# A two-block transformer layer stack on one core: the engines' instruction order drawn up on a detailed timeline instead of a simple clock

## The chip, the core and the metric

The kernel runs on one core of one Trainium2 chip. A core has a matrix engine (TensorE, called PE in the profile, with its weight loads shown apart as PEld), VectorE (DVE), ScalarE (ACT), GpSimd (POOL) and SyncE (SP), which here issues every transfer from memory. The metric is the device time of one execution in microseconds (us); lower is better. The time given for a kernel is the median of several executions.

## What is computed

256 tokens of width 1024 pass through a first block and then through two layers of a second block, all in 32-bit floats:

```
x = first_block(x, ...)       # norm, one wide projection, three mixers side by side
                              # (gated recurrence, sparse attention, gated linear attention),
                              # gated merge, output projection, feed-forward
return second_block(x, c, ctx, ...)   # two layers over 256 tokens and 256 context tokens:
                              # half feed-forward, mixer (attention + gating, or pooling +
                              # neighbourhood attention), half feed-forward
```

In the second block every norm is scaled and shifted by vectors that come from a small input through a large matrix:

```
m = jnp.split((sc @ ada_w[li] + ada_b[li])[:, None, :], N_MOD, axis=-1)
```

Each layer uses 9 such vectors for the tokens and 9 for the context. Nearly all the arithmetic is in products with weight matrices, each of which is read once.

## The kernel before

**Matmuls.** A weight tile is 128 by 1024 floats (512 KB). `wload` (L62 to L78) loads it into `wraw`, ScalarE rounds it to a shorter format (`wh`, L71), and VectorE computes what the rounding left out (`wl`, L72). `mm3` (L99) then multiplies with both parts: for each 128-column piece of a tile one product with `wh` (L104) and one with `wl` (L105), and after these the product of `wh` with the small part of the activations (L108). A full tile gives 24 matmuls. `wraw`, `wh` and `wl` have three buffers each, the PSUM tiles four of tag `mm` and four of tag `at` (L96).

**Work beside it.** The modulation vectors are made on VectorE. `Ada.chunk` (L1059) loads 128 by 512 floats into `araw` and multiplies and sums them twice (`junk`, L1066), once for the tokens and once for the context. There are 288 chunks. They are "fillers": `wload` calls `fill` at a rate that the stage sets, so that some chunks are written down after each weight tile. `junk` shares the tag `silu`, with two buffers, with the feed-forward's intermediate results.

**Norms.** A norm sums squares (L148 to L152), adds them up over partitions with small matmuls (`rstd`, L164), takes a power on GpSimd (L116), spreads the result with transposes (L173), and scales the activations on VectorE and ScalarE (L185 to L195) before the next projection can start. `stagger` (L198) splits the tokens in halves at most such places, so that one half's matmuls run while the other half is normed. The last mixer (`out_proj` with 256 tokens) doesn't split; there two weight tiles are loaded ahead, with their `wl` computed on GpSimd.

**Attention.** `weave` (L218) writes down a step of an attention chain after each so many dense matmul units.

**What sets the order.** The Python code writes instructions down in one sequence, the program order. When the `TileContext` (L2012) is left, a scheduler walks a clock of its own and draws up a list for each engine: when an engine is free on that clock, it gets the instruction that stands earliest in program order among those whose inputs are ready and whose tile has a buffer. Buffers of a tag are handed out in program order. On the chip each engine then runs its list in that order, and semaphores make an instruction wait for its inputs. So program order is a priority, and the scheduler's clock decides what overtakes what.

## Time and profile before

| quantity | value |
|---|---|
| median of 3 executions | 2399.82 us |
| lowest, highest | 2396.43, 2409.7 us |
| the profiled execution: its time | 2397.43 us |
| the profiled execution: its span, first to last instruction | 2395.7 us |
| TensorE busy | 2356.5 us, 98% of the span |
| VectorE busy | 1715.2 us, 72% |
| ScalarE busy | 1049.3 us, 44% |
| GpSimd busy | 183.7 us, 8% |
| mean clock granted to TensorE, share of full | 0.990 |
| moved by transfers | 398.91 MB |

Busy time is the time in which at least one instruction of an engine was running. The times of rows are those of the profiled execution, which took 1.7 us more than its span. [...]

### The profile page before, as it was taken

How to read it: one execution, taken by the hardware profiler on the slowest of the kernel's cores; microseconds unless marked ns; L12 is line 12 of the kernel's file. 1: busy time of each engine (PE TensorE's matmuls, PEld its weight loads, DVE VectorE, ACT ScalarE, POOL GpSimd, SP SyncE). 2: the span in 40 equal slices, each digit the busy share in tenths (PEclk: the TensorE clock that was granted, in tenths of full speed). 3: DMA queues.
4: the chain of work that ended last, by engine and by line, in shares of the span. 5: the costliest groups of instructions: out<-in, count | busy, mean ns of one | idle time of the engine just before them, and what ended most of it. 6: DMA issues, size and time to landing. Idle time of an engine off the chain costs nothing.

```text
span 2395.7 us, 38691 instructions
## 1 busy us (share of the span) xinstructions
PE 2356.5 (98%) x14647; PEld 2072.7 (87%) x14647; DVE 1715.2 (72%) x3622; ACT 1049.3 (44%) x1879; POOL 183.7 (8%) x208
## 2 busy tenths in 40 slices
PE   8999999999999999999999999999999999998999
PEld 8888988999999988888778888889888888878999
DVE  6986798679899965448787765666865655856555
ACT  4542576565444532236755322224422223665443
POOL 1100130010000000013321000000100000101000
PEclk8999999999999999999999999999999999998999
DMA  7884534367887754555324644544654543633655
GB/s 215 271 270 129 154 100 127 124 191 226 255 260 215 243 183 139 149 168 167 99 67 140 209 150 133 159 146 141 205 163 123 167 137 106 185 100 117 190 181 156
DMA packets 158022, 398.91 MB, mean 167 GB/s; under 512 B 27099, under 2 KB 41339, under 8 KB 157835
## 3 DMA queue, kind: packets, MB, share of 16 engines
q1 hardware_dynamic: 157835, 396.44, 53.1%
q8 instruction: 115, 1.88, 0.3%
q14 instruction: 72, 0.59, 0.1%
HBM read 389.56 MB, written 5.77 MB: 165 GB/s over the span
## 4 chain that ended last, share of the span: by engine, by line
PE 88%; DVE 5%; DMA 2%; ACT 2%; POOL 2%; issue 1%; SPq 0%; ACTq 0%; DVEq 0%; POOLq 0%
PE ps_mm L104 24%; PE ps_mm L105 24%; PE ps_mm L108 24%; PE ps_mm L1208 2%; PE ps_mm L1210 2%; PE ps_mm L1209 2%; DVE wl L72 1%; PE ps_at L1325 1%; PE ps_mm L1457 1%; PE ps_mm L578 1%; PE ps_at L1314 1%; ACT wh L71 1%; DMA wraw<-in_up 1%; DVE junk L1066 1%; PE ps_mm L1687 1%
## 5 line engine op out<-in xcount | busy, mean ns | idle before, releaser
L71 ACT CAST wh<-wraw 128x1024 fp32r<-128x1024 f32 (+2 forms) x603 | 604.7, 1004 | 754.6 <-PE ps_mm L108 383.1
L72 DVE TENSOR_TENSOR wl<-wraw,wh 128x1024 fp32r<-128x1024 f32 (+2 forms) x601 | 706.6, 1177 | 294.7 <-ACT wh L71 287.9
L104 PE MATMUL ps_mm<-zh,wh 128*128 128x256 f32 (+1 forms) x2568 | 769.2, 324 | 7.9 <-ACT wh L71 3.9
L105 PE MATMUL ps_mm<-zh,wl 128*128 128x256 f32 (+1 forms) x2568 | 766.8, 323 | 3.1 <-DVE wl L72 3.0
L104 PEld LDWEIGHTS ps_mm<-zh,wh 128*128 128x128 f32 x2568 | 492.5, 192 | 61.8 <-issue 12.0
L105 PEld LDWEIGHTS ps_mm<-zh,wl 128*128 128x128 f32 x2568 | 493.2, 192 | 45.4 <-DVE wl L72 5.3
L108 PE MATMUL ps_mm<-zl,wh 128*128 128x256 f32 (+1 forms) x2568 | 455.7, 320 | 0.0
L108 PEld LDWEIGHTS ps_mm<-zl,wh 128*128 128x128 f32 x2568 | 381.6, 190 | 38.1 <-issue 1.0
L1066 DVE SCALAR_TENSOR_TENSOR junk<-araw,cs 128x512 f32<-128x512 f32 x576 | 391.0, 693 | 11.1 <-DMA araw<-in_ada_w 3.7
L104 PE MATMUL ps_mm<-hh,wh 128*128 128x256 f32 (+1 forms) x1021 | 312.3, 328 | 0.9 <-ACT wh L71 0.9
L105 PE MATMUL ps_mm<-hh,wl 128*128 128x256 f32 (+1 forms) x1021 | 310.9, 327 | 1.1 <-DVE wl L72 1.1
L104 PEld LDWEIGHTS ps_mm<-hh,wh 128*128 128x128 f32 x1021 | 192.2, 188 | 21.1 <-ACT wh L71 1.1
L105 PEld LDWEIGHTS ps_mm<-hh,wl 128*128 128x128 f32 x1021 | 192.3, 188 | 19.8 <-DVE wl L72 1.5
L108 PE MATMUL ps_mm<-hl,wh 128*128 128x256 f32 (+1 forms) x1021 | 193.6, 327 | 0.0
L263 ACT ACTIVATE silu<-ps_mm 128x256 f32<-128x256 f32 (+1 forms) x124 | 58.7, 473 | 303.8 <-PE ps_mm L108 287.9
L108 PEld LDWEIGHTS ps_mm<-hl,wh 128*128 128x128 f32 x1021 | 156.2, 188 | 18.3 <-DVE hl L266 0.3
L1155 DVE SCALAR_TENSOR_TENSOR X<-ps_mm,adac,X 128x256 f32<-128x256 f32 x128 | 61.8, 483 | 129.2 <-PE ps_mm L108 127.6
L264 DVE TENSOR_TENSOR silu<-silu,ps_mm 128x256 f32<-128x256 f32 (+1 forms) x124 | 65.9, 531 | 110.9 <-PE ps_mm L108 110.1
L116 POOL TENSOR_TENSOR rs_v<-rs_v,power 128x2 f32<-128x2 f32 (+1 forms) x17 | 22.6, 1331 | 1068.3 <-ACT wh L71 692.1
L1208 PE MATMUL ps_mm<-wh,zh 128*128 128x512 f32 (+1 forms) x224 | 87.0, 389 | 0.0
L1209 PE MATMUL ps_mm<-wh,zl 128*128 128x512 f32 (+1 forms) x224 | 85.4, 381 | 0.0
L1210 PE MATMUL ps_mm<-wl,zh 128*128 128x512 f32 (+1 forms) x224 | 85.3, 381 | 0.0
(379 smaller groups left out, 2611.1 us busy)
## 6 DMA issues: line engine op xcount, KB each, us to landing
wraw<-in_up SPq DMA_DIRECT2D x204, 512.0 KB, 3.7
araw<-in_ada_w SPq DMA_DIRECT2D x288, 256.0 KB, 3.5
wraw<-in_w_in_t SPq DMA_DIRECT2D x72, 512.0 KB, 4.0
wraw<-in_dn SPq DMA_DIRECT2D x79, 448.0 KB, 3.2
wraw<-in_f_up SPq DMA_DIRECT2D x44, 512.0 KB, 4.1
wraw<-in_dn SPq DMA_DIRECT2D x40, 512.0 KB, 3.7
wraw<-in_ev_in SPq DMA_DIRECT2D x26, 512.0 KB, 4.3
wraw<-in_w_br SPq DMA_DIRECT2D x24, 512.0 KB, 3.6
```

Of the source, the lines that this page charges most:

```text
L71: nc.scalar.copy(h[:, :cols], raw[:, :cols])
L72: (low or nc.vector).tensor_tensor(out=l[:, :cols], in0=raw[:, :cols], in1=h.bitcast(F32)[:, :cols], op=ALU.subtract)
L104: nc.tensor.matmul(out, wh, ah, start=start and k == 0, stop=False)
L105: nc.tensor.matmul(out, wl, ah, start=False, stop=False)
L108: nc.tensor.matmul(out, wh, al, start=False, stop=stop and k == n - 1)
L263: nc.scalar.activation(g, pair[0], AF.Silu)
L264: nc.vector.tensor_tensor(out=g, in0=g, in1=ps, op=ALU.mult)
L1066: nc.vector.scalar_tensor_tensor(out=junk, in0=raw, scalar=1.0, in1=self.cs[:, s, h * 512:(h + 1) * 512], op0=ALU.mult, op1=ALU.mult, accu ...
L1155: self.nc.vector.scalar_tensor_tensor(out=X[:, m, :], in0=ps, scalar=self.ada.c[l][:, j, m, s:s + 1], in1=X[:, m, :], op0=ALU.mult, op1=AL ...
L1208: nc.tensor.matmul(ps[i], z.zh[:, k, tk], wh[:, w], start=k == 0, stop=False)
L1209: nc.tensor.matmul(ps[i], z.zl[:, k, tk], wh[:, w], start=False, stop=False)
L1210: nc.tensor.matmul(ps[i], z.zh[:, k, tk], wl[:, w], start=False, stop=k == 7)
```

## The change

One argument is added. The kernel's own code, its tiles, buffers and instructions are those of before.

```
     out = nc.dram_tensor("out", (P, 8, 256), F32, kind="ExternalOutput").ap()
-    with tile.TileContext(nc) as tc:
+    with tile.TileContext(nc, schedule_with_timeline_sim=True) as tc:
         build(tc, D, out)
```

The scheduler's rule stays: earliest in program order among those that are ready. What changes is the clock on which it decides who is ready and who is free. The simple clock gives each instruction one duration on its engine. The detailed one follows an instruction through its engine's sequencer, its waits, its execution and the signal that it sends, and lets transfers share the transfer engines.

## Rows read from the trace of the kernel before

**Rows 1.** The page: span, busy time by engine, chain that ended last.

```profile
span 2395.7 us, 38691 instructions
...
PE 2356.5 (98%) x14647; PEld 2072.7 (87%) x14647; DVE 1715.2 (72%) x3622; ACT 1049.3 (44%) x1879; POOL 183.7 (8%) x208
...
PE 88%; DVE 5%; DMA 2%; ACT 2%; POOL 2%; issue 1%; SPq 0%; ACTq 0%; DVEq 0%; POOLq 0%
```

**Rows 2.** Windows of 60 us: PE, PEld, DVE, ACT, POOL, clock, DMA, GB/s.

```profile
0.00:60.00 60.00, 52.26 (x343) 49.60 (x344) 40.38 (x86) 28.42 (x47) 7.58 (x22) 0.86 0.71 215
60.00:120.00 60.00, 56.15 (x378) 50.78 (x377) 55.71 (x125) 34.99 (x48) 6.22 (x7) 0.94 0.84 270
...
480.00:540.00 60.00, 57.28 (x462) 56.38 (x461) 44.93 (x81) 36.35 (x70) 11.80 (x14) 0.97 0.62 193
...
600.00:660.00 60.00, 60.00 (x501) 59.79 (x500) 50.94 (x103) 27.10 (x42) 0.00 (x0) 1.00 0.82 255
...
720.00:780.00 60.00, 57.92 (x482) 57.16 (x481) 54.42 (x118) 28.85 (x45) 1.39 (x2) 1.00 0.72 218
...
900.00:960.00 60.00, 60.00 (x260) 48.65 (x259) 36.05 (x73) 14.98 (x19) 0.00 (x0) 1.00 0.47 144
...
1260.00:1320.00 60.00, 56.71 (x372) 51.23 (x372) 48.26 (x101) 35.22 (x69) 9.03 (x10) 0.97 0.47 145
...
2160.00:2220.00 60.00, 52.15 (x401) 50.66 (x401) 40.06 (x77) 32.45 (x66) 9.67 (x7) 0.89 0.43 132
...
2340.00:2395.70 55.70, 52.09 (x434) 51.70 (x432) 28.18 (x37) 20.45 (x29) 0.00 (x0) 1.00 0.50 152
```

**Rows 3.** Waits of PE: for whom, total us, times, longest.

```profile
PE ps_at L173 <- POOL rs_v L116: 6.1, 5, 2.0
PE ps_at L164 <- DVE acc L152: 5.6, 1, 5.6
PE ps_mm L104 <- ACT wh L71: 4.9, 6, 2.0
PE ps_mm L105 <- DVE wl L72: 4.1, 8, 0.9
```

**Rows 4.** Timeline of the first 14 us: start, length, engine, operation.

```profile
1.59 0.56 POOL L826 MEMSET gatt<- 128x256 f32 x2
...
10.43 1.04 ACT L71 CAST wh<-wraw 128x1024 fp32r<-128x1024 f32 x1 [0.30 <-DMA wraw<-in_w_in_t]
...
12.81 0.87 DVE L185 SCALAR_TENSOR_TENSOR zt<-X,ng,ps_at 128x256 f32<-128x256 f32 x2 [1.35 <-PE ps_at L173]
...
13.61 1.22 DVE L72 TENSOR_TENSOR wl<-wraw,wh 128x1024 fp32r<-128x1024 f32 x1
```

**Rows 5.** Timeline around the norm after the last mixer, 2186 to 2196 us.

```profile
2187.17 0.43 DVE L152 TENSOR_TENSOR acc<-acc,sq 128x256 f32<-128x256 f32 x1
...
2189.74 4.84 POOL L72 TENSOR_TENSOR wl<-wraw,wh 128x1024 fp32r<-128x1024 f32 x2 [123.77 <-ACT wh L71]
2190.01 2.36 DVE L152 TENSOR_TENSOR acc<-acc,sq 128x256 f32<-128x256 f32 x1 [1.55 <-ACT sq L151]
...
2192.69 2.17 DVE L152 TENSOR_TENSOR acc<-acc,sq 128x256 f32<-128x256 f32 x1
```

**Rows 6.** Groups of instructions: busy us, mean ns, idle before.

```profile
L71 ACT CAST wh<-wraw 128x1024 fp32r<-128x1024 f32 (+2 forms) x603 | 604.7, 1004 | 754.6 <-PE ps_mm L108 383.1
L72 DVE TENSOR_TENSOR wl<-wraw,wh 128x1024 fp32r<-128x1024 f32 (+2 forms) x601 | 706.6, 1177 | 294.7 <-ACT wh L71 287.9
...
L1066 DVE SCALAR_TENSOR_TENSOR junk<-araw,cs 128x512 f32<-128x512 f32 x576 | 391.0, 693 | 11.1 <-DMA araw<-in_ada_w 3.7
...
L1066 DVE DVE_READ_ACCUMULATOR junk<-araw,cs 128x1 f32 x576 | 47.6, 83 | 0.0
```

**Rows 7.** Windows of line 1066 alone: DVE busy (instructions), clock, DMA, GB/s.

```profile
180.00:240.00 60.00, 16.51 (x50) 0.97 0.41 128
240.00:300.00 60.00, 0.00 (x0) 1.00 0.51 154
```

## Prediction

> **What bounds the kernel now.** I read the page first. PE is busy in 2356.5 of 2395.7 us and makes up 88% of the chain that ended last [rows 1]. No instruction is added or taken away, so this work stays: an order can only act on the 39.2 us in which PE stands still, on the time in which its clock is low after such stops, and on new stops.
>
> The windows of 60 us say where the 39.2 us lie [rows 2]. The first window has 7.74 (60 less 52.26), the one from 2160 us has 7.85, and the last has 3.61. At the first and the last there is little beside the one chain of loads, norm or output, so I call these three, 19.2 us together, set by the dependencies (with one exception below). The other 20.0 us are open to an order: 3.85 in 60 to 120, 2.72 in 480 to 540, 2.08 in 720 to 780, 3.29 in 1260 to 1320, and the rest in pieces. [...] In the windows between, as 900 to 960, PE is busy throughout at 1.00, and no order can speed that up.
>
> The waits of PE name the causes [rows 3]: the power on GpSimd in a norm (6.1 us), the sums of squares (5.6 in one wait), and weights that came late, rounded part 4.9 and rest 4.1.
>
> **How far the order can move.** The trace shows that the lists do not follow program order. GpSimd clears tiles of the linear attention (L826) at 1.59 us, though the code writes them after most projections [rows 4]. But buffers bind it. The fillers (L1066) take 16.51 us of VectorE in 180 to 240 and none in 240 to 300 [rows 7]: the next ones are written after the first tiles of tag `silu` of the second block, and that tag is handed out in program order. Weight tiles can't run more than three ahead, PSUM tiles four of a tag. So the new clock can swap neighbours; it can't move work between stages.
>
> **The change, part by part.**
>
> *Misjudged arrivals.* An example is in the start: ScalarE has the second weight tile rounded at 11.47 us (10.43 + 1.04). VectorE stands still until 12.81, does two products of the norm, and only then takes the rest `wl`, 1.22 us, after which the other products of the norm follow [rows 4]. The list was drawn up on a clock on which the tile came later. Had `wl` come first, it would have run in the 1.35 us of idle time, and the norm's chain would be up to 1.2 us shorter. A clock that describes transfers more closely may repair this: between 0 and -1.2 us, and I take -1.2. The late weights, 9.0 us together [rows 3], are of the same kind. A better clock could remove all of them; equally, one transfer that lands later on the chip than on any clock leaves them. I take a third, -3.0.
>
> *Non-preemptive fillers.* An engine's list can't be interrupted on the chip. Where a chain step becomes ready just after a filler was placed, it waits for the rest of it. A chunk takes 1.32 us of VectorE (16.51 us for 25 pairs of product and accumulator read, two pairs a chunk, [rows 7]), a `wl` 1.18 [rows 6]. At the five norms where PE waited for GpSimd [rows 3], two VectorE steps stand in the chain. If the new order puts one half of 1.2 us more before half of these steps, that is 5 x 0.6 = 3.0 us; the bounds are a gain of the 6.1 us waited now and a loss of 5 x 2 x 1.32 = 13.2. I take +3.0, nearer to zero, since the same rule of priority holds.
>
> *The norm after the last mixer.* There VectorE's sums (L152) take 2.36 and 2.17 us instead of 0.43, while GpSimd runs two `wl` in 4.84 us [rows 5]. Without the collision the chain is 2.36 + 2.17 - 2 x 0.43 = 3.7 us shorter, half of the 7.85 us of idle time there. The clock of this window is 0.89, up to 6.6 us more [rows 2]. This is the exception named above. The order could keep the two apart, by putting GpSimd's work before or after. But both `wl` are ready as soon as ScalarE has rounded the tiles, GpSimd has nothing else to do, and the rule starts what is ready. So I take 0 here; the bounds are -10.3 (3.7 and 6.6) and nothing.
>
> [...]
>
> *PE's own list.* Swapping matmuls that are ready leaves their sum as it is: nothing, covered by PE's own backlog of up to three tiles. Where that cover is gone, it shows as one of the waits above.
>
> *Sum.* -1.2 - 3.0 + 3.0 + 0 = -1.2 us, from 2397.4 (span 2395.7 and 1.7 around it) to 2396.2. The median of the runs was 2.4 us above the profiled one, so I expect a median of 2399.
>
> **The rivals.**
>
> *Slower: VectorE's lists get too full in the tight stages.* In 60 to 120 VectorE is busy 55.71 of 60, in 600 to 660 50.94, in 720 to 780 54.42 [rows 2]; a tile passes PE in 24 x 60/501 = 2.87 us. If the detailed clock fills an engine's queue ahead of time, it decides sooner and with fewer candidates ready, so fillers overtake `wl` more often. What it takes: three buffers give a tile 3 x 2.87 = 8.6 us from rounding to its last matmul; rounding, rest and matmuls need 1.00 + 1.18 + 2.87 = 5.05 [rows 2, 6]. So 3.5 us are spare: two chunks (2.64) in front of a `wl` are hidden, three (3.96) are not. From there each tile that is late costs its whole further delay, and a VectorE at 90% hardly catches up. The stages 60 to 180 and 540 to 840 pass 420/2.87 = 146 tiles; one in six late by a chunk is 24 x 1.32 = 32 us, 2431. It decides from nine such tiles on (12 us). For it: PE already waits for `wl` eight times. Against it: each wait is 0.9 us or shorter [rows 3], and PE is not idle at all in 600 to 660.
>
> [...]
>
> [...]
>
> *Nothing happens: the orders come out nearly the same.* Then 2399.8 stays. For it: long stretches of full tiles with one possible order.
>
> **How the numbers follow.** A difference of 0.5%, 12 us, is about what a measurement of this kernel can tell from none. Within it: 0.44, of which 0.06 for orders nearly alike; the likeliest case has its own range, 2389 to 2411. Slower: 0.31, nearly all from full lists on VectorE; I give it more than the sum suggests since new stops have no upper bound, while only 27 to 37 us can be won. Faster: 0.25. The range from 2382 to 2432 leaves out one in ten on each side: below, more than half of all that an order can give; above, more than one late tile in six.
>
> **What would show it.** Right: PE busy near 2356 us, idle time between 30 and 50 us, fillers in the same stages as now, the stops at 0 to 22 and 2185 to 2200 us still there. The first step is right if `wl` of the second tile starts before 12 us. Fullness shows as waits of PE for `wl` and `wh` of more than 15 us together, in 60 to 180 and 540 to 840. Wrong would be a changed PE busy time, long new waits in the attention stages (PE for `n`, `t` or `ysb`), which I count as hidden, or fillers that appear in 240 to 540.

## The result, and the profile after

The changed kernel takes 2442.1 us (median of 4 runs, 2438.6 to 2452.7) against 2403.5 for the kernel before: a ratio of 1.0175, 95% interval 1.0151 to 1.0198. It is slower by 1.75%; the forecast was no change, and the time lies 10 us above the range.

The page of the kernel after, to be held against [rows 1]:

```profile
span 2438.2 us, 38759 instructions
...
PE 2370.3 (97%) x14647; PEld 2083.6 (85%) x14647; DVE 1710.3 (70%) x3622; ACT 1051.1 (43%) x1879; POOL 172.8 (7%) x208
```

PE runs the same 14647 matmuls, and the other engines as many instructions as before; the 68 more are semaphore instructions. The span is 42.5 us longer: PE stands still for 67.9 us instead of 39.2 (28.7 more), and its busy time grows by 13.8. The clock can account for the second part: the mean granted clock fell from 0.990 to 0.982, at most 0.008 x 2438 = 20 us.

The waits of PE, kernel after, to be held against [rows 3]:

```profile
PE ps_mm L104 <- ACT wh L71: 12.3, 18, 1.5
PE ps_at L164 <- DVE acc L152: 5.7, 2, 5.5
PE ps_at L173 <- POOL rs_v L116: 5.2, 3, 2.2
PE ps_mm L104 <- ACT zh L194: 5.2, 3, 2.9
PE ps_mm L1208 <- ACT zh L190: 5.1, 2, 2.6
PE ps_mm L105 <- DVE wl L72: 4.9, 7, 1.4
PE ps_mm L104 <- ACT zh L190: 4.7, 3, 1.9
PE ps_at L1314 <- ACT n8u L1286: 3.6, 3, 2.0
```

Rows of the kernel before that [rows 3] doesn't have:

```profile
PE ps_mm L104 <- ACT zh L190: 2.8, 3, 1.1
...
PE ps_mm L104 <- ACT zh L194: 1.1, 1, 1.1
```

Two things have grown: the rounded weights `wh` come late 18 times instead of 6, and PE waits longer for steps on ScalarE, the norm's tiles `zh` (15.0 us in the rows above, 3.9 before) and the even layer's attention (`n8u`, 3.6; `n`, 1.9 before). The rest of a weight, `wl`, is hardly later than before at line 105.

To see where the time went I cut both traces at the same places, the matmuls of line 173 (and 890) with which a norm begins to broadcast its result. The windows that matter, kernel before (length, PE busy, granted clock, DMA share, GB/s): the first projections, the first block's attention, the stage with tiles of 256 columns, the even layer, the odd layer's mixer.

```profile
0.00:236.70 236.70, 225.09 (x1486) 0.94 0.70 224
236.70:511.70 275.00, 271.58 (x2060) 1.00 0.44 136
511.70:779.20 267.50, 263.99 (x2183) 0.99 0.74 231
...
1099.20:1303.50 204.30, 198.28 (x1083) 0.99 0.35 110
...
2055.40:2197.90 142.50, 135.80 (x747) 0.98 0.44 135
```

The same five, kernel after:

```profile
0.00:243.50 243.50, 227.26 (x1542) 0.96 0.70 220
243.50:515.30 271.80, 269.73 (x2045) 0.99 0.44 139
515.30:799.10 283.80, 272.72 (x2218) 0.98 0.71 223
...
1123.40:1337.90 214.50, 200.98 (x1063) 0.94 0.33 101
...
2093.60:2241.20 147.60, 134.97 (x728) 0.95 0.38 118
```

The stage with 256 columns is 16.3 us longer, the even layer 10.2, the first projections 6.8, the odd mixer 5.1. (A cut is no fence: 35 matmuls more lie in the longer 256-column stage, so a few of its us are moved work.) The long stretches of 512 columns between them, 1072 us before, lose 8 us together, and the end gains 0.8.

What happens in the 256-column stage, at its start. Start and end of three weight tiles in PE, us (from both traces, each matmul matched with its tile by its place in PE's list):

| tile | before | after |
|---|---|---|
| `ps_mm_1175` | 518.55 to 525.12 | 517.47 to 531.91 |
| `ps_mm_1176` | 519.90 to 528.19 | 517.71 to 532.03 |
| `ps_mm_1183` | 528.62 to 531.70 | 519.29 to 532.75 |

The new list has all three begun by 519.29 us, and they end within 0.84 us of each other. The three slots of `wh` and `wl` are taken for 13 us and then come free together. What follows, timeline of the kernel after (start, length, engine, operation, idle time before it):

```profile
531.95 0.38 ACT L263 ACTIVATE silu<-ps_mm 128x256 f32<-128x256 f32 x1 [5.91 <-PE ps_mm L108]
532.23 1.98 ACT L71 CAST wh<-wraw 128x1024 fp32r<-128x1024 f32 x2
...
533.00 2.44 DVE L1740 SCALAR_TENSOR_TENSOR n<-n,ng,ps_at 128x256 f32<-128x256 f32 x6 [0.22 <-PE ps_at L173]
...
533.32 0.38 PE L104 MATMUL ps_mm<-zh,wh 128*128 128x256 f32 x1 [0.35 <-ACT wh L71]
...
534.26 0.38 PE L104 MATMUL ps_mm<-zh,wh 128*128 128x256 f32 x1 [0.56 <-DVE n L1740]
534.39 1.04 ACT L71 CAST wh<-wraw 128x1024 fp32r<-128x1024 f32 x1
...
535.48 0.38 PE L104 MATMUL ps_mm<-zh,wh 128*128 128x256 f32 x1 [0.84 <-ACT wh L71]
...
536.63 0.58 PE L105 MATMUL ps_mm<-zh,wl 128*128 128x256 f32 x1 [0.77 <-DVE wl L72]
```

ScalarE stood still for 5.91 us and now has three tiles to round in 3.2 us; VectorE takes the first `wl` only after six steps of the norm, 2.44 us. The three matmuls of line 104 are the first of three further tiles, and only then comes the second matmul of the first one: PE's list again begins a tile, leaves it, begins the next, and stands still for 2.5 us in four waits.

In PE's list of the kernel before, PE leaves an unfinished tile of the weight stream for another one 157 times, in the new list 473 times (counted in the lists themselves); of the 533 tiles of `mm3`, 56 and 214 have a matmul of another PSUM tile between their own. Of the 157 and 473 changes, 12 and 59 stand in the 256-column stage.

### The profile page after: what moved, and what is told of

It is laid out like the page before. It is cut to its first block, busy times and chain, and to the rows that moved or that the text cites. A ratio compares the mean times of both kernels' runs of the same rounds, so it can differ in the third digit from the quotient of the medians.

```text
span 2438.2 us, 38759 instructions
## 1 busy us (share of the span) xinstructions
PE 2370.3 (97%) x14647; PEld 2083.6 (85%) x14647; DVE 1710.3 (70%) x3622; ACT 1051.1 (43%) x1879; POOL 172.8 (7%) x208
## 4 chain that ended last, share of the span: by engine, by line
PE 63%; DVE 2%; ACT 2%; DMA 1%; issue 0%; POOL 0%; ACTq 0%; DVEq 0%; POOLq 0%
PE ps_mm L104 17%; PE ps_mm L105 17%; PE ps_mm L108 17%; PE ps_mm L1208 2%; PE ps_mm L1209 2%; PE ps_mm L1210 2%; PE ps_at L1325 2%; PE ps_mm L1457 1%; PE ps_at L1314 1%; ACT wh L71 1%; PE ps_mm L1687 1%; DVE wl L72 1%; DMA wraw<-in_up 0%; DVE acc L152 0%; PE ps_at L164 0%
```

## The experiments

All of them use one helper. `lists` builds the program a second time under either scheduler and returns each engine's order; `hold` makes an engine keep an order while the scheduler draws up everything else around it (order only, no waits are added).

```
def hold(tc, engines, order=None, only=None, change=None):
    traced = list(tc.nc.cur_bb.bb.instructions)
    for e in engines:
        mine = [traced[k] for k in order[e]]   # order None: as the program names them
        ...
        for a, b in zip(mine, mine[1:]):
            tc.add_manual_dep(b, a.name, NoSync)   # order alone
```

The theories: **D**, VectorE's list (the rival of the prediction); **S**, SyncE's or ScalarE's list; **P**, PE's own list, which mixes tiles; later **F**, the new lists fit a clock that is not the chip's and lose wherever they run; and **T**, the program's constants were fitted to the simple clock's lists.

### One engine's list exchanged

```
 e1  TileContext(nc, schedule_with_timeline_sim=True):   hold(tc, ["PE"], lists(False))
 e2  the same flag:    hold(tc, ["DVE", "Activation", "Pool", "SP"], lists(False))
 e3  TileContext(nc):  hold(tc, ["PE"], lists(True))
 e4  the same flag as e1:  hold(tc, ["DVE"], lists(False))
```

e1: 

> The detailed simulation draws up every list but TensorE's, which is held in the order of the kernel before. Theory P (the loss is in TensorE's own list: matmuls of two or three tiles are mixed, so weight tiles and PSUM tiles come free in bursts): the loss goes, 2395 to 2412 us, TensorE idle 35 to 48 us, waits for wh together under 8 us. Theory D (the loss is in VectorE's list: fillers ahead of the low halves wl) and theory S (the loss is in the lists of SyncE or ScalarE): nothing is won back, 2430 to 2450 us, idle above 60 us.

e2: 

> The reverse: the lists of VectorE, ScalarE, GpSimd and SyncE are held in the order of the kernel before, and the detailed simulation draws up TensorE's alone. Theory P: the loss stays whole, 2430 to 2455 us, idle above 60 us. Theories D and S: the loss goes, 2395 to 2412 us. A time in the middle (2413 to 2429) would say that the loss is in the fit between the lists and not in one of them.

e3: 

> The kernel before (simple clock) with TensorE's list alone held in the order of the changed kernel; the simple clock draws up the other four around it. Theory P: as slow as the changed kernel, 2425 to 2455 us. Theories D and S: as the kernel before, 2395 to 2412 us.

e4: 

> The changed kernel with VectorE's list alone held in the order of the kernel before. Theory D, the rival of the prediction (fillers stand ahead of the low halves): 2395 to 2415 us. Theories P and S: 2430 to 2455 us, no nearer to the kernel before than the changed kernel is.

Measured: e1 2459.4 us, ratio 1.0248 (1.0229 to 1.0266); e2 2474.1, 1.0324 (1.0277 to 1.0371); e3 2475.9, 1.0325 (1.0295 to 1.0355); e4 2496.7, 1.0408 (1.0391 to 1.0425). All four are slower than both kernels, and above every theory's figure. D and S miss at once: with VectorE's list of before the kernel loses 55 us more, and e2 should have been at 2412 or below. P in its simple form misses too, by e1. But every exchange brings a loss of its own, so these four runs can't say what any single list was worth. What e1's waits show, however, is half of P:

```profile
PE ps_at L1314 <- ACT n L1286: 8.2, 3, 5.4
PE ps_at L600 <- DVE t L591: 7.4, 2, 5.4
PE ps_at L497 <- DVE t L142: 6.9, 2, 4.5
```

The waits for `wh` at line 104 are down to 1.5 us in e1 and those for `wl` at line 105 to 2.8; in e3, which has the new PE list, they are 20.9 and 25.3. So late weights do come with PE's new list. But PE's old list stands attention steps where the new lists of the other engines do not have their inputs yet. The lists of one scheduler fit each other, and a kernel with a whole engine's list from the other scheduler is 2.5 to 4.1% slower than the kernel before.

### Mixing forbidden, and mixing alone

```
 e5  flag on:   hold(tc, ["PE"], only=dense)     # matmuls that write a ps_mm tile, as the program names them
 e6  flag off:  hold(tc, ["PE"], only=dense)
 e7  flag off:  hold(tc, ["PE"], lists(False), change=mixed)
 # mixed: where two whole tiles stand one behind the other, the last 8 matmuls of
 # the first and the first 8 of the second alternate
 e8  flag off:  hold(tc, ["PE", "DVE", "Activation", "Pool", "SP"])
```

e5: 

> The detailed simulation draws up everything, but TensorE's matmuls of the weight stream (those that write a ps_mm tile) are queued in the order in which the program names them, so that it cannot leave one tile unfinished and begin the next; the attention's and norms' matmuls stay free to move between them. Theory P (mixed tiles hold all three weight slots and free them together): most of the loss goes, 2398 to 2418 us, waits for wh and wl together under 9 us. Theory F (the detailed simulation's lists fit each other by a clock that is not the chip's, and the mixing is only a sign of it): 2430 to 2470 us, as when TensorE's list alone was exchanged.

e6: 

> The same queueing of the weight stream's matmuls with the simple clock. The kernel before leaves a dense tile for another 157 times, this one 79 times. Theory P: 2385 to 2399 us, less waiting for wh and wl. Theory F: no difference that can be told, 2396 to 2410 us.

e7: 

> The kernel before, with one thing added by hand: wherever two whole tiles of mm3 stand one behind the other in TensorE's list, the last 8 matmuls of the first alternate with the first 8 of the second; the simple clock draws up the other four lists around it. Theory P: mixing alone costs, 2415 to 2455 us, waits for wh and wl together over 20 us. Theory F: mixing alone costs nothing that counts, 2396 to 2408 us.

e8: 

> No scheduler's choice at all: every engine's list is the order in which the program names its instructions. It tells how much of either list's time a scheduler's freedom is worth. Theory P: TensorE's list is unmixed (77 switches), but the other engines' steps stand behind work that is not needed yet, 2430 to 2520 us, with few waits for wh and wl. Theory F: far slower than either, over 2480 us.

Measured: e5 2449.9 us, 1.0198 (1.0173 to 1.0223); e6 2422.6, 1.0086 (1.0063 to 1.0109); e7 2425.7, 1.0087 (1.0063 to 1.0111); e8 4597.4, 1.9142. P for the whole kernel falls: e5 is no faster than the changed kernel, and e6, with less mixing, is 21 us slower than the kernel before. In e6 PE waits 10.2 us for `zh` at line 104 (3.9 before), 2.6 of it in the even layer, which grows by 7.3: some of the 157 changes of tile seem to bridge such waits. The odd mixer grows by 4.2 with 0.7 us more of stops, so that is mostly clock (0.96 granted, 0.98 before). Neither theory had that. e7 has 5435 changes of tile and loses 21 us by its ratio (25 by the medians); its time is in P's range, but the waits for `wh` and `wl` that P expects there, over 20 us, are 11.3 in the rows of lines 104, 105 and 481. In the 256-column stage, where the new list costs 16.3 us with 59 changes, e7's added changes, all at the ends of tiles, cost 1.2. So the number of changes is not the cost; where they stand is. The largest single part of e7's loss, 12.6 us in the even layer, comes with only 0.5 us more of stops: it is clock (0.93 granted, 0.99 before; last section).

e8 lies far beyond what either theory had in mind, though F's "over 2480" holds; P's "few waits for wh and wl" does not. It shows what a scheduler's freedom is worth here: PE waits 814.8 us for `wh` at line 104 alone, 296 times, and its mean granted clock is 0.794.

The table cuts the profiled executions at the same places; a field is the stage's length less that of the kernel before, in brackets the part of it in which PE stood still, in us.

| | projections | attention 1 | 256 columns | even layer | odd mixer | rest |
|---|---|---|---|---|---|---|
| after | +6.8 (4.6) | -3.2 (-1.4) | +16.3 (7.6) | +10.2 (7.5) | +5.1 (5.9) | +7.3 |
| e1 | +20.2 (16.1) | +12.5 (7.4) | +2.9 (2.7) | +22.8 (13.3) | +0.8 (0.3) | -0.9 |
| e2 | +13.6 (8.3) | +9.6 (8.6) | +5.2 (4.6) | +35.9 (10.1) | +0.8 (2.4) | +7.3 |
| e3 | +15.7 (9.7) | +4.8 (4.3) | +22.8 (16.2) | +28.0 (17.4) | -3.2 (0.9) | +11.1 |
| e4 | +22.7 (13.8) | +13.0 (6.7) | +7.6 (7.8) | +31.0 (13.6) | +5.9 (4.5) | +10.1 |
| e5 | +15.6 (11.3) | -2.6 (-3.4) | +5.3 (2.7) | +9.7 (11.4) | +9.1 (5.0) | +9.3 |
| e6 | +4.8 (5.7) | +0.1 (0.1) | -0.6 (0.6) | +7.3 (2.8) | +4.2 (0.7) | +4.9 |
| e7 | +7.4 (3.0) | +6.2 (4.7) | +1.2 (0.8) | +12.6 (0.5) | -0.4 (-0.4) | +5.1 |

Read down the columns: in the 256-column stage the changed kernel and e3, which have the same PE list, lose by far the most; forbidding the mix (e5) takes 11 us off. The even layer loses in every row, whatever is changed, in e7 without more stops.

### P confined to one stage, and T

```
 e9   flag on:   hold(tc, ["PE"], only=staged)               # dense, PSUM tiles 1140 to 1767: the 256-column stage
 e10  flag off:  hold(tc, ["PE"], lists(True), only=staged)
 e11  flag off, e12 flag on:
-EV, EV2, EV3, OD, OD2, GL, NS = 1.9, 1.75, 1.1, 1.8, 1.0, 1.95, 0.83
+EV, EV2, EV3, OD, OD2, GL, NS = (0.94 * r for r in (1.9, 1.75, 1.1, 1.8, 1.0, 1.95, 0.83))
```

e9: 

> The changed kernel, with TensorE's matmuls of the weight stream queued as the program names them in one stage alone: the one whose tiles are 256 columns wide (512 to 779 us in the kernel before, longer by 16.6 us in the changed kernel). Theory P, confined to this stage after the whole-kernel trial (a weight serves only one tile of 256 columns here, so mixed tiles starve it): that stage's excess falls to 3 to 7 us and the time to 2427 to 2436 us. Theory F (mixing is only a sign): the stage keeps over 12 us of excess and the time stays at 2438 to 2455 us.

e10: 

> The reverse: the kernel before, with the weight stream's matmuls of that one stage queued in the changed kernel's order; the simple clock draws up everything else. Theory P: the stage grows by 12 to 23 us and the time is 2412 to 2424 us, with the waits for wh and wl inside the stage. Theory F: the stage grows by less than 5 us, 2396 to 2406 us.

e11: 

> The kernel before with the seven constants that say how many attention steps the program names per weight tile multiplied by 0.94. Theory T (these constants are fitted to the lists of the simple clock, so that any other lists lose in the attention stages): slower than before, 2410 to 2440 us, and about as slow as the detailed simulation with the same constants. Theory F (the detailed simulation's lists are worse whatever the program): 2396 to 2410 us, 30 us or more below the detailed simulation with the same constants.

e12: 

> The changed kernel with the same seven constants multiplied by 0.94. Theory T: within 15 us of the simple clock with the same constants, apart from the 11 us or so that the 256-column stage costs, 2420 to 2445 us. Theory F: 30 us or more above the simple clock with the same constants, 2430 to 2460 us.

Measured: e9 2429.1 us, 1.0132 (1.0111 to 1.0153); e10 2413.2, 1.0076 (1.0049 to 1.0103). Both times are as P expects; in e9 the stage keeps 7.4 us, where P had 3 to 7. The stage in e9, then in e10, and the waits of PE within it in e10:

```profile
523.10:798.00 274.90, 268.74 (x2218) 0.99 0.74 230
```

```profile
515.10:794.70 279.60, 266.19 (x2183) 0.98 0.71 221
```

```profile
PE ps_mm L105 <- DVE wl L72: 6.7, 4, 2.3
PE ps_mm L104 <- ACT wh L71: 3.3, 5, 1.1
```

With the same 2218 matmuls in the stage, e9 takes 8.9 us less than the changed kernel, and no wait for a weight is left in it. In e10 the same 2183 matmuls as before take 12.1 us more, 9.9 of them standing still, all of it in this stage: the other stages of e10 are within 0.5 us of the kernel before but for 3.2 in the projections. So in this stage PE's order of the weight stream, which is what these two runs exchange, is the cause: worth 10 to 13 us undone (by ratios and by medians) and 15 to 18 added. With e7, where mixing at the ends of tiles costs the stage 1.2 us, this points at tiles that are begun and left.

e11: 2420.1 us, 1.0104 (1.0079 to 1.0128); e12: 2448.1, 1.0205 (1.0176 to 1.0234). Constants 6% lower cost the simple clock 22 us by the medians (25 by the ratio); the detailed simulation is 6 or 7 slower, within its intervals. The gap between the two shrinks from 42 to about 24 (1.0205 - 1.0104 = 1.0%). T is right that the simple clock loses, but wrong that both are then about equally slow, and e12 is 3 us above its range; F's 30 us of gap is missed too.

### The even layer, additivity, and the other side of T

```
 e13  flag off:  hold(tc, ALL, lists(True), only=within(tc, (2284, 2706)))         # the even layer, all five engines
 e14  flag on:   hold(tc, ALL, lists(False), only=within(tc, (0, 1140), (2284, 2706), (3887, 4164)))
                 hold(tc, ["PE"], only=staged)
 e15, e16: as e11 and e12 with 1.06 for 0.94
```

e13: 

> The kernel before, with all five engines' lists of the changed kernel held in the even layer's attention alone (1099 to 1304 us); the simple clock draws up everything else. If the excess of that stage lies in its own lists: the stage grows by 8 to 14 us, 2407 to 2416 us, with the stops at the projections' zh (line 1208) and at line 1314 there again. If the excess is carried in from the stages ahead (weights fetched later, a later filler): the stage grows by less than 4 us, 2396 to 2403 us.

e14: 

> The changed kernel with two repairs: all five lists of the kernel before held in the stages with attention (0 to 512, 1099 to 1304 and 2055 to 2198 us by the kernel before), and the weight stream unmixed in the 256-column stage. If the stages' losses add up (19 us in the attention stages, 12 us in the 256-column stage): 2407 to 2416 us. Theory F in its strong form (the detailed simulation's lists lose wherever they run): the excess moves to the seams and to the other stages, 2418 to 2440 us. If nothing but these stages mattered: 2398 to 2406 us.

e15: 

> The kernel before with the seven constants (attention steps named per weight tile) multiplied by 1.06 instead of 0.94. Theory T (they are fitted to the simple clock's lists): slower on this side too, 2408 to 2435 us. If 0.94 was only a step in the wrong direction: 2385 to 2402 us.

e16: 

> The changed kernel with the same constants multiplied by 1.06. Theory T: the detailed simulation is no worse off than with the original constants and perhaps better, 2425 to 2443 us, within 20 us of the simple clock with the same constants. Theory F: 30 us or more above the simple clock with the same constants, 2440 to 2465 us.

Measured: e13 2417.5 us, 1.0062 (1.0039 to 1.0084), 9 to 20 us; the time is a little over the forecast, and the stage grows by 15.8 us instead of 8 to 14. The stops of the changed kernel are there again, at the same lines; the stage and the waits within it, e13:

```profile
1103.20:1323.30 220.10, 206.70 (x1063) 0.91 0.31 99
```

```profile
PE ps_mm L104 <- ACT zh L194: 3.6, 1, 3.6
PE ps_at L1314 <- ACT n8u L1286: 3.0, 2, 2.0
PE ps_mm L1208 <- ACT zh L190: 2.6, 1, 2.6
```

PE stands still for 7.4 us more than before in it, in the changed kernel 7.5. So this stage's stops come from its own lists; they are not carried in. The other half of its 15.8 us is clock, 0.91 instead of 0.99. How one of these stops comes about, ScalarE's list in the changed kernel ahead of PE's 2.56 us at line 1208, which ended at 1129.64 us:

```profile
1125.13 1.04 ACT L71 CAST wh<-wraw 128x1024 fp32r<-128x1024 f32 x1
1126.07 0.59 ACT L1377 COPY n<-ps_mm 128x512 f32<-128x512 f32 x1
...
1126.96 0.62 ACT L1229 ACTIVATE hsq<-n 128x512 f32<-128x512 f32 x1
...
1128.67 0.62 ACT L1229 ACTIVATE hsq<-n 128x512 f32<-128x512 f32 x1
1129.19 0.70 ACT L190 CAST zh<-zt 128x256 fp32r<-128x256 f32 x2
...
1129.64 0.59 PE L1208 MATMUL ps_mm<-wh,zh 128*128 128x512 f32 x1 [2.56 <-ACT zh L190]
```

A rounding, an eviction and two squares, 2.87 us, stand in ScalarE's list between the norm's steps, while PE's list has the projection that needs `zh` next. e13 held the lists of all five engines, so it doesn't tell which of them the stage's loss needs.

e14: 2414.7 us, 1.0056 (1.0036 to 1.0075), as forecast if the stages' losses add up. The two repairs take 27 us off the changed kernel (2442.1 - 2414.7), and 13 are left. The profiled execution, at 2424.3 us the longest of nine, shows what kind of loss is left: PE stands still for 48.0 us (39.2 before, 67.9 in the changed kernel), in the even layer for 6.3 (6.0 before). Yet that layer is 15.1 us longer than before:

```profile
1111.80:1331.20 219.40, 213.11 (x1090) 0.92 0.32 100
```

There the repair brought the stops back to those of before, and in this execution the clock took more than they had cost (last section).

e15: 2416.9 us, 1.0072 (1.0041 to 1.0103); e16: 2442.5, 1.0179 (1.0151 to 1.0208). On this side, too, the simple clock loses, 16 us, and the detailed simulation nothing; the gap is 1.1%, 26 us, between T's 20 and F's 30. The kernel before stands at the best of three settings for its own lists; the changed kernel's time hardly depends on them.

No version was faster than the kernel before.

## Why the prediction was wrong

**What can be won or lost.** That the order acts on PE's idle time and on the clock alone is what the result shows (28.7 and 13.8 us). The signs named for it did not hold: busy time moved from 2356 to 2370, idle time is outside 30 to 50 us. That 27 to 37 us can be won, as the sentence on the chances has it, and with it the lower end of the range, no run shows: every other order that was run, the changed kernel's and those of the sixteen experiments, took longer, by 0.6% (e14) to 91% (e8).

**How far the order can move.** "It can't move work between stages" was wrong for the fillers. Line 1066 alone, kernel before and then kernel after (VectorE busy):

```profile
0.00:60.00 60.00, 3.95 (x13) 0.86 0.71 215
```

```profile
0.00:60.00 60.00, 13.97 (x41) 0.91 0.80 239
...
180.00:240.00 60.00, 0.00 (x0) 0.91 0.25 74
```

The 16.51 us of [rows 7] in 180 to 240 moved ahead. None moved into 240 to 540, as said. What the move cost is not shown. It ends in the projections, which are 6.8 us longer, 4.6 of it in stops, and there PE waits for `wh` 7.9 us instead of 3.4 (lines 104, 373 and 479). In the same stretch, 0 to 240 us, ScalarE's roundings wait for transfers of weights for 27.2 us instead of 8.8. A transfer into `wraw` starts when VectorE's `wl` has freed the buffer (the queue of transfers waits 96.3 us for `wl` in this stretch, 73.6 before), and the fillers load their own chunks beside it, so both a VectorE with more fillers and more transfers at a time could be behind this. No run undid the fillers alone.

**Misjudged arrivals, -1.2 and -3.0.** The `wl` of the second tile starts at 13.78 us, not before 12 and not earlier than the 13.61 of [rows 4]. Late `wh` and `wl` at lines 104 and 105 went from 9.0 us [rows 3] to 17.2 instead of to 6.0.

**Non-preemptive fillers, +3.0.** The norms' waits for GpSimd went from 6.1 us [rows 3] to 5.2: small, with the other sign, well inside the bounds. But the term counted VectorE's steps alone. Where the norms' waits grew is ScalarE: PE's waits for `zh` (lines 104 and 1208) went from 3.9 us to 16.2, by 12.3. In the one of these stops that was followed (at 1129.64 us) the norm's steps stand behind other work: the kind of delay was right there, and the engine was not. (A chunk, too, is dearer than the 1.32 us taken from [rows 7]: by [rows 6] it is (391.0 + 47.6)/288 = 1.52, which moves the bounds and not the sign.)

**The norm after the last mixer, 0.** Right. Kernel after, to be held against [rows 5]:

```profile
2231.64 2.34 POOL L72 TENSOR_TENSOR wl<-wraw,wh 128x1024 fp32r<-128x1024 f32 x1 [126.32 <-ACT wh L71]
2231.91 4.99 DVE L152 TENSOR_TENSOR acc<-acc,sq 128x256 f32<-128x256 f32 x2 [1.00 <-ACT sq L151]
```

The same collision, and PE waits 5.5 us instead of 5.6.

**PE's own list, nothing.** This is the step that failed most plainly. "Swapping matmuls that are ready leaves their sum as it is" holds for the matmuls and not for what they hold: a tile that is begun and left keeps its slots of `wh`, `wl` and PSUM, tiles that are open together end together, and the roundings for the next three start late and in a row (in the case above slots held for 13 us, ends within 0.84 us, roundings of 3.2 us). The backlog of up to three tiles that was named as cover is used up by just this. In the 256-column stage it costs 10 to 18 us (e9, e10). In the even layer the new lists together cost 9 to 20 (e13), part of it clock; the one stop that was followed has a norm's consumers next in PE's list while ScalarE's list has other work ahead of their input. The first I had priced at nothing, and the second not looked for on ScalarE.

**The slower rival.** Its time, 2431, was the nearest of all; as far as the runs show, that is luck. Its sign, over 15 us of waits for `wh` and `wl` together in 60 to 180 and 540 to 840, did not come: all such rows of the kernel after have 6.1 us in the first stretch and 4.7 in the second, 10.8 together, after 4.6 in the kernel before. (The 17.2 us above are those of lines 104 and 105 over the whole kernel.) Full lists on VectorE are not ruled out as a part of it: e4 exchanged VectorE's whole list and with it broke the fit between lists, and a late `wh` does not clear VectorE, as its buffer `wraw` waits for `wl`. In the 256-column stage PE's order alone accounts for most of the loss (e9); in the projections the question is open.

**The range.** Its upper end took one late tile in six in the weight stages and nothing in the attention stages. Those I counted as hidden; by the table they hold 12.1 us of the 42.5 (attention 1, even layer and odd mixer), and the projections 6.8.

**What stays open.** Why the detailed simulation prefers to leave a tile was not shown, nor where its clock and the chip's part. Of the 42 us (1.75%), mixing in the 256-column stage has 10 to 13; the lists of the stages with attention come next, with some 14 to 17 of the 27 that e14 takes back; 13 belong to no single place that was tried. Cut another way, some 16 us of the gap go when the program's constants are moved (e11 to e16), because the simple clock loses its fit. That a part of the loss is this fit, and not worse lists as such, is argued and not shown: only one common factor was tried, and no constants were sought for the detailed simulation.

## What to carry to other kernels

An order of ready work is not free to change where the work holds buffers: count how many tiles an engine's new list has open at once, and compare with the slots. A kernel's constants can be fitted to one scheduler's lists, as here, where 6% either way cost the simple clock 16 to 22 us; a second scheduler should be compared with constants of its own. And a whole engine's list taken from one scheduler and set among the lists of the other was, in all four trials, worse than either.

## What the runs showed of the hardware

In the even layer the clock can cost as much as the stops themselves, or more: e13 is 15.8 us longer there, 7.4 of it in stops, e14 15.1 with 0.3. Windows of 20 us in the even layer of the changed kernel (PE busy, granted clock):

```profile
1160.00:1180.00 20.00, 16.13 (x76) 0.91 0.40 127
...
1220.00:1240.00 20.00, 20.00 (x71) 0.74 0.05 18
```

From 1220 to 1240 us PE is busy throughout, and yet its mean granted clock is 0.74: in windows of 1 us it reads 0.50 from 1223 to 1232 us and 1.00 before 1222 and after 1233. That is up to 5 us lost (0.26 x 20), an estimate, after a stretch with stops of 0.2 to 2.0 us.

One and the same stop need not have the same consequence. In the even layer of the kernel before and of e14, which has the same lists there, PE waits 1.71 us for `n` at line 1314 (it ends at 1222.81 and at 1235.40 us). The windows around it, kernel before and then e14:

```profile
1220.00:1240.00 20.00, 18.06 (x102) 1.00 0.05 16
1240.00:1260.00 20.00, 19.99 (x111) 1.00 0.31 93
```

```profile
1220.00:1240.00 20.00, 18.29 (x86) 0.91 0.22 67
1240.00:1260.00 20.00, 20.00 (x64) 0.50 0.00 1
1260.00:1280.00 20.00, 20.00 (x103) 0.82 0.22 61
```

After the stop PE is busy almost throughout in both. The kernel before is granted 1.00 throughout; e14 has 0.50 for 20 us and 0.82 for 20 more, up to 13.6 us lost (0.50 x 20 + 0.18 x 20, an estimate). e7 has the same stop of 1.71 us and then granted clocks of 0.53 and 0.70. What decides it is not shown; it is most of the 15.1 us by which this layer is longer in e14 and of the 12.6 in e7.

Runs of one and the same program differ in this too: of 8 runs of the kernel before beside e9, one took 2392.9 us at a mean clock of 0.993; of 9 beside e5, one took 2407.8 at 0.987. The difference, 14.9 us, is what 0.006 of the clock makes of 2400 (14.4). So a stage's length from a single profile can carry 10 us or more of this, an estimate from these rows, and its idle time is the better sign.
